# Layer 2's second feed-forward product by seven block products, in groups of six features, with the residual stream added in DRAM

## The chip, the cores and the metric

The kernel runs on one core of a Trainium2 chip. TensorE (PE) multiplies matrices into PSUM, VectorE (DVE), ScalarE (ACT) and GpSimd (POOL) do the rest, and SyncE (SP) issues transfers; ACT and POOL issue some too. Sixteen DMA engines move the data. The metric is the device time of one execution in microseconds (us).

## The reference

One step of a two-layer backbone with residual width 1024: 512 latent tokens and 128 context tokens. Each layer has a mixer and a gated feed-forward part of 2816 hidden units:

```python
def conv_ffn(h, w_up, conv_w, conv_b, w_down):
    a, b = jnp.split(h @ w_up, 2, axis=-1)
    a = dwconv(a, conv_w, conv_b)
    return (jax.nn.silu(a) * b) @ w_down

x = x + g1 * (mix @ p['w_out'][i])
h = rmsnorm(x, p['norm_ffn'][i]) * (1.0 + sc2) + sh2
x = x + g2 * conv_ffn(h, ...)          # after layer 2: y = rmsnorm(x, p['final_norm'])
```

The first product (`w_up`) makes two times 2816 columns, the depthwise convolution runs along the tokens, and the second product (`w_down`) brings the 2816 gated values back to 1024. The gate `g2` has one column for latent and one for context tokens.

## The kernel before

**Layout.** Activations are held with channels on the 128 partitions and tokens along the free dimension: 512 latent tokens, a gap of two columns, 128 context tokens, so 642 columns (`NT`). The residual stream `x` is four tiles of two times 642 columns. The 2816 hidden units are 22 "features" of 128 (`NF`).

**Three matmuls for one.** Every operand of a large product is split into a rounded part and a residue (`fp32r` high and low); `mm3` then issues high x high, low x high and high x low. A split is a cast on ACT and a subtraction on DVE (`split_w`, `split_op`, `Blocks.split`).

**First product (`up_unit`).** The tokens are cut into two halves of 320 (`SPARTS`, `ST`; the gap left out) and the channels into two halves of four. With the two columns of `w_up` that belong to one feature (its `a` and its `b`), this is a two by two block product, done with seven block products instead of eight, of four channel blocks each: 7 x 4 x 3 = 84 matmuls of 320 columns for a feature. `Blocks` and `combine` make the sums and differences of activation blocks, once for the layer; `block_weights` those of the weights for each feature, two of them by a DMA that accumulates (issued on POOL, L591). The seven weight operands use eight half rooms (`op_room`).

**Gate (`give`).** A feature's `a` goes through the convolution (ACT L677, twice DVE L679), SiLU (ACT L683) and the product with `b` (DVE L684), and is split into the tiles of `g` (ACT L686, DVE L687).

**Second product (`project_out`).** The features come in three groups of 8, 7 and 7 (`FGROUPS`). After the up units of a group, each of the eight output blocks takes the group's features as plain products, in two token parts of 384 and 258 columns, and the result times `g2` is added to `x` in SBUF (`residual`, DVE L446). In the last group this carries the final norm with it: squares (ACT L437), their sum over channels, a scaling by the final gain (`scaled`, ACT L2010), and at the end the scaling by the inverse root (`final`, L2020: GpSimd for the first token part, DVE for the second).

**Buffers.** The pool `slots` has 20 slots of 642 x 2 values per partition. In layer 2's feed-forward part 14 hold blocks of activations, 4 hold `x`, 2 the outputs `ab` of the up units. Another pool of 8 slots holds raw blocks at first and the split gated features of one group after that. Raw weights share three buffers (`wr`), the accumulated weight sums two (`t13`).

**Order.** The code is written in program order. The framework's planner gives each engine its own order: it estimates when an instruction's inputs and buffers are there, and of those that are ready takes the one that is written first. Each engine's queue, and that of each transfer issuer, is then fixed and worked off in that order. In the trace weights are so loaded and split about one unit ahead, and matmuls of the next product stand between those of the present one where the plan had a wait.

## Time and profile before

| | us |
|---|---|
| median of 3 runs (1879.08 to 1884.51) | 1882.99 |
| the profiled execution | 1880.43 |
| its span, first to last instruction | 1878.7 |
| layer 2's first up units to its first down stage | 1440 to 1535 |
| the three down stages (8, 7, 7 features) | 1535 to 1592, 1679 to 1729, 1815 to 1867 |
| the tail after the last matmul of the product | 1867 to 1878.7 |

A row of a group reads: line, engine, operation, output and input tiles with their shapes, number, busy time and mean duration of one in nanoseconds, and the idle time before it with what ended it. A row of stages gives the busy time and the number of instructions of each engine, the clock that TensorE was granted (1.00 is full) and the mean busy share of the sixteen DMA engines. A row of the timeline gives start and duration in us. Consecutive matmuls overlap, so the distance of their starts is what one costs.

### The profile page before, as it was taken

The numbers are of one execution on the slowest core, as the hardware profiler recorded it, in microseconds if no ns is written. First come the engines' busy times: TensorE is split into PE (matmuls) and PEld (weight loads), VectorE is DVE, ScalarE is ACT, GpSimd is POOL, SyncE is SP. The second block draws the span as 40 slices with busy tenths as digits, with TensorE's granted clock in tenths as the row PEclk, the third lists the DMA queues.
The fourth block names the chain that finished last, engine by engine and source line by source line (L and its number), as shares of the span: only waits on it lengthen the run. The fifth ranks groups of instructions, "written<-read, shape, count | busy, mean of one in ns | idle before, by whom it ended". The sixth has DMA issues, their size and how long they took to land.

```text
span 1878.7 us, 31471 instructions
## 1 busy us (share of the span) xinstructions
PE 1788.3 (95%) x12052; PEld 1665.0 (89%) x12052; DVE 1374.1 (73%) x2896; ACT 848.1 (45%) x1678; POOL 311.4 (17%) x349
## 2 busy tenths in 40 slices
PE   5899999999888899999999999999999999999997
PEld 1578999998667899999999998977799999999997
DVE  5755666667887989886887888976778874774874
ACT  3555443433232436633634635445526651552653
POOL 2323442324544210000000003200000000000001
PEclk9899999999989999999999999999999999999999
DMA  8332112224544641555556563411242552552631
GB/s 292 128 104 77 36 57 74 67 72 138 176 168 139 234 141 53 143 186 141 138 183 168 130 217 138 140 53 40 91 180 62 146 152 57 146 139 74 160 90 57
DMA packets 86066, 234.20 MB, mean 125 GB/s; under 512 B 9080, under 2 KB 20728, under 8 KB 85786
## 3 DMA queue, kind: packets, MB, share of 16 engines
q1 hardware_dynamic: 66112, 192.45, 30.9%
q0 software_dynamic: 5760, 20.97, 6.7%
q10 hardware_dynamic: 14042, 18.76, 2.9%
q8 instruction: 95, 1.56, 0.3%
q14 instruction: 57, 0.47, 0.1%
HBM read 215.61 MB, written 16.54 MB: 124 GB/s over the span
## 4 chain that ended last, share of the span: by engine, by line
PE 72%; DVE 13%; ACT 3%; POOL 3%; issue 2%; DMA 2%; POOLq 0%; DVEq 0%; ACTq 0%
PE mm L310 10%; PE mm L312 10%; PE mm L311 10%; PE bx L310 4%; PE bx L311 4%; PE bx L312 4%; PE bv L312 2%; PE bv L310 2%; PE bv L311 2%; PE tr L1009 2%; PE fx L1395 1%; PE YT L1176 1%; PE Y L1174 1%; PE Q L1168 1%; PE o L1872 1%
## 5 line engine op out<-in xcount | busy, mean ns | idle before, releaser
L579 ACT CAST cwh<-wr 128x512 fp32r<-128x512 f32 x200 | 119.6, 621 | 144.8 <-PE bx L311 45.9
L304 ACT CAST wwh<-wr 128x1024 fp32r<-128x1024 f32 (+1 forms) x100 | 101.3, 1013 | 175.8 <-PE mm L311 133.9
L580 DVE TENSOR_TENSOR cwl<-wr,cwh 128x512 fp32r<-128x512 f32 x200 | 133.8, 686 | 36.2 <-ACT cwh L579 36.0
L305 DVE TENSOR_TENSOR wwl<-wr,wwh 128x1024 fp32r<-128x1024 f32 (+1 forms) x100 | 122.2, 1223 | 39.4 <-ACT wwh L304 38.6
L310 PE MATMUL mm<-h0h,wwh 128*128 128x384 f32 (+2 forms) x448 | 148.5, 331 | 0.5 <-DVE d L850 0.2
L446 DVE SCALAR_TENSOR_TENSOR x<-mm,mod,x 128x128 f32<-128x128 f32 (+3 forms) x192 | 77.5, 436 | 95.0 <-PE mm L312 94.8
L311 PE MATMUL mm<-h0l,wwh 128*128 128x384 f32 (+2 forms) x448 | 140.1, 313 | 0.0
L591 POOL DMA_DIRECT2D t<-in_w_up x40 | 34.5, 864 | 633.4 <-DMA t<-in_w_up 150.0
L312 PE MATMUL mm<-h0h,wwl 128*128 128x384 f32 (+2 forms) x448 | 139.3, 311 | 0.0
L257 DVE SCALAR_TENSOR_TENSOR mjunk<-mraw,crow 128x512 f32<-128x512 f32 x192 | 125.3, 685 | 1.9 <-DMA mraw<-in_w_modT 1.4
L310 PE MATMUL od<-owh,h2h 128*128 128x256 f32 x320 | 97.0, 305 | 0.1
L679 DVE SCALAR_TENSOR_TENSOR cv<-ab,par,cv 128x641 f32<-128x641 f32 x88 | 77.7, 883 | 25.2 <-ACT cv L677 24.4
L312 PE MATMUL od<-owh,h2l 128*128 128x256 f32 x320 | 91.5, 289 | 2.1 <-DVE h2l L430 1.3
L311 PE MATMUL od<-owl,h2h 128*128 128x256 f32 x320 | 90.5, 284 | 0.0
L310 PEld LDWEIGHTS mm<-h0h,wwh 128*128 128x128 f32 x448 | 85.3, 190 | 3.7 <-issue 1.8
L1139 POOL TENSOR_TENSOR am<-a,msk 128x512 fp32r<-128x512 f32 x60 | 73.0, 1225 | 92.4 <-PE Q L1168 81.2
L311 PEld LDWEIGHTS mm<-h0l,wwh 128*128 128x128 f32 x448 | 84.8, 189 | 0.5 <-issue 0.2
L312 PEld LDWEIGHTS mm<-h0h,wwl 128*128 128x128 f32 x448 | 84.5, 189 | 0.1
L726 DVE SCALAR_TENSOR_TENSOR cv<-mm,par,cv 128x382 f32<-128x382 f32 (+2 forms) x96 | 52.1, 544 | 32.5 <-ACT cv L720 31.7
L579 ACT CAST cwh<-t 128x512 fp32r<-128x512 f32 x80 | 48.0, 622 | 47.5 <-PE bx L311 17.3
L437 ACT ACTIVATE sq<-x 128x320 f32<-128x320 f32 (+4 forms) x63 | 31.5, 501 | 78.7 <-DVE x L446 64.8
L310 PEld LDWEIGHTS od<-owh,h2h 128*128 128x128 f32 x320 | 60.4, 189 | 4.5 <-issue 4.2
(555 smaller groups left out, 6170.7 us busy)
## 6 DMA issues: line engine op xcount, KB each, us to landing
wr<-in_w_mod SPq DMA_DIRECT2D x48, 512.0 KB, 4.6
wr<-in_w_up SPq DMA_DIRECT2D x48, 512.0 KB, 4.2
mraw<-in_w_modT SPq DMA_DIRECT2D x40, 512.0 KB, 5.5
t<-in_w_up SPq DMA_DIRECT2D x80, 256.0 KB, 3.1
t<-in_w_up POOLq DMA_DIRECT2D x40, 512.0 KB, 5.5
wr<-in_w_in SPq DMA_DIRECT2D x28, 512.0 KB, 3.3
wr<-in_w_dn SPq DMA_DIRECT2D x32, 448.0 KB, 3.5
wr<-in_w_up SPq DMA_DIRECT2D x40, 256.0 KB, 3.7
```

The lines of the kernel that those rows point to most:

```text
L257: nc.vector.scalar_tensor_tensor(out=junk, in0=w[:, c : c + 512], scalar=1.0, in1=rows[m][:, c0 + c : c0 + c + 512], op0=ALU.mult, op1=ALU ...
L304: nc.scalar.copy(hi[:, :K], src)
L305: nc.vector.tensor_tensor(out=lo[:, :K], in0=src, in1=hi[:, :K].bitcast(F32), op=ALU.subtract)
L310: nc.tensor.matmul(ps, l[0](k), r[0](k), start=start, stop=False, skip_group_check=more)
L311: nc.tensor.matmul(ps, l[0](k), r[1](k), start=False, stop=False, skip_group_check=more)
L312: nc.tensor.matmul(ps, l[1](k), r[0](k), start=False, stop=stop, skip_group_check=more)
L446: nc.vector.scalar_tensor_tensor(out=xt[:, a:b], in0=ps[:, a - c0 : b - c0], scalar=mcol(layer, ch, d, m), in1=xt[:, a:b], op0=ALU.mult, o ...
L579: nc.scalar.copy(hi, src)
L580: nc.vector.tensor_tensor(out=lo, in0=src, in1=hi.bitcast(F32), op=ALU.subtract)
L679: nc.vector.scalar_tensor_tensor(out=t[:, c0:c1], in0=ar[:, c0 + s_ : c1 + s_], scalar=w[i], in1=t[:, c0:c1], op0=ALU.mult, op1=ALU.add)
L726: nc.vector.scalar_tensor_tensor(out=t[:, c0:c1], in0=p[:, c0 + s_ - a : c1 + s_ - a], scalar=w[i], in1=t[:, c0:c1], op0=ALU.mult, op1=ALU ...
L1139: eng.tensor_tensor(out=v(out), in0=v(a32), in1=msk[:, lv, :, None, :].broadcast_to([P, 2, 2, P]), op=ALU.mult)
```

## The change

In layer 2 the features now come in groups of 6, 6, 6 and 4 (`BGROUPS`). For the first three the second product is a two by two block product as well: token halves of 320, the group's even and odd features, and two neighbouring output blocks. Seven block products of three feature pairs each (7 x 3 x 3 = 63 matmuls of 320 columns) give one pair of output blocks; there are four such pairs for a group.

- `Gated` takes the place of `Act` for these groups. `put` writes the gated feature into a raw tile by two operations (512 and 128 columns); after each odd feature `combine` makes and splits the blocks a11, a12, a22 and the sums s1 to s4.
- `down_weights` makes the seven weight operands of an output pair: four loads on SP's queue, two accumulating transfers on POOL's, two sums on DVE and seven splits.
- `down_blocks` does the products, gates them (`ga` on what comes out with a plus, `ngate` with a minus) into a tile `o` out of `slots`, and adds `o` to the residual in DRAM by an accumulating transfer on POOL's queue. `o` waits for a slot, and its gap is cleared by a memset on POOL.
- `x` is stored to DRAM (`x2s`) on ACT's queue after layer 2's second norm, and its four slots go to `Gated`. It is read back into the other pool after the second unit of the last group, on SP's queue.
- The last group of four features goes through `project_out` as before, with the final norm.

Layer 1 keeps its groups and its products.

```diff
+BGROUPS = ((0, 6), (6, 6), (12, 6), (18, 4))
...
     def split_op(src):
-        hi, lo = op_room()
+        hi, lo = (t_[:, : src.shape[1], :] for t_ in op_room())
...
+    class Gated:
+        PAIRS = (("a12", "a22"), ("s3", "s1"), ("s4", "s2"))
...
+        def room(self, k):
+            p_ = None if k == 0 and self.first else self.pool
+            for i in range(3):
+                self.t[i, k] = slot(f"{self.s}p", (P, 4, ST), F32R, p_)
+            if k % 2 == 0:
+                self.a11[k] = slot(f"{self.s}q", (P, 4, ST), F32R, p_)
+
+        def put(self, f, src):
+            k, i = divmod(f, 2)
+            if i == 0:
+                self.now = slot(f"{self.s}r", (P, 4, ST), pool=self.pool)
+            r = self.now[:, 2 * i : 2 * i + 2, :].rearrange("p n t -> p (n t)")
+            src(0, 512, r[:, :512])
+            src(PO, NT, r[:, 512:])
+            if i:
+                self.room(k)
+                self.combine(k)
...
+        def combine(self, k):
+            TT, STT = nc.vector.tensor_tensor, nc.vector.scalar_tensor_tensor
+            a11, a21, a12, a22 = (self.now[:, i, :] for i in range(4))
+            h_, l_ = self.parts("a11", k)
+            nc.scalar.copy(h_, a11)
+            self.split(0, k, self.now[:, 2:4, :])
+            TT(out=l_, in0=a11, in1=h_.bitcast(F32), op=ALU.subtract)
+            TT(out=a11, in0=a11, in1=a21, op=ALU.subtract)
+            TT(out=a21, in0=a22, in1=a21, op=ALU.subtract)
+            self.split(1, k, self.now[:, 0:2, :])
+            STT(out=a22, in0=a11, scalar=-1.0, in1=a22, op0=ALU.mult, op1=ALU.subtract)
+            STT(out=a12, in0=a22, scalar=-1.0, in1=a12, op0=ALU.mult, op1=ALU.subtract)
+            self.split(2, k, self.now[:, 2:4, :])
...
+    def down_weights(layer, p, f0, n, pool):
+        TT = nc.vector.tensor_tensor
+        m = n // 2
+        w_a, w_b = (A["w_dn"][layer, 2 * p + i][:, 128 * f0 : 128 * (f0 + n)] for i in range(2))
+        eo = lambda ap: ap.rearrange("p (k i c) -> p i k c", i=2, c=128)
+        t13 = pool.tile([P, 1024], F32, tag="t13", name=nm("t13"), bufs=2)[:, : 128 * n].rearrange("p (i k c) -> p i k c", i=2, c=128)
+        for i, w_ in enumerate((w_a, w_b)):
+            nc.sync.dma_start(t13[:, i], eo(w_)[:, 0])
+        for i in range(2):
+            nc.gpsimd.dma_start(t13[:, i], eo(w_b)[:, i], accum_op=ALU.add)
...
+    def down_blocks(xd, G, layer, f0, n, ngate, pool):
+        m = n // 2
+        for p in range(4):
+            o = slot("o")
+            nc.gpsimd.memset(o[:, :, 512:514], 0.0)
+            ws = down_weights(layer, p, f0, n, pool)
...
+            X, Y = bank("d", "dx"), bank("mm", "dy")
+            product(X, "a11", True)
+            q1 = keep("q1", X, SPARTS[0], ga)
+            product(Y, "a12", True)
+            give(0, Y, SPARTS[0], ga, q1)
+            product(X, "s2", False)
+            u2 = keep("u2", X, SPARTS[0], nb)
+            V = bank("d", "dv")
+            product(V, "s1", True)
+            q5 = keep("q5", V, SPARTS[1], nb)
+            product(X, "s3", False)
+            give(1, X, SPARTS[1], nb, q5)
+            product(V, "s4", False)
+            give(1, V, SPARTS[0], nb, u2)
+            product(X, "a22", False)
+            for a, b, c0 in SPARTS[1]:
+                nc.scalar.activation(o[:, 0, a:b], X[:, c0 : c0 + b - a], AF.Copy, scale=ga[0 if a < PO else 1])
+            nc.gpsimd.dma_start(xd[:, 2 * p : 2 * p + 2, :], o, accum_op=ALU.add)
...
+                if xd is not None and not by_blocks and f == f0 + 1:
+                    for i in range(4):
+                        x[i] = slot("xb", pool=gpool)
+                        nc.sync.dma_start(x[i], xd[:, 2 * i : 2 * i + 2, :])
+            if by_blocks:
+                down_blocks(xd, g, layer, f0, n, ngate, pool)
+                continue
...
+            elif xd is not None:
+                for i in range(4):
+                    nc.scalar.dma_start(xd[:, 2 * i : 2 * i + 2, :], x[i])
```

More of the change, by code (lines that the diff above doesn't have):

```diff
@@ new lines, in ffn_blocks @@
+    def ffn_blocks(x, B, pool, layer, then, post, gstack, pre, lanes=((),) * 4, xd=None):
+        gpool = B.pool
+        groups = BGROUPS if xd is not None else FGROUPS
+        if xd is not None:
+            ngate = perm.tile([P, KD, 2], F32, tag="ngate", name="ngate")
+            nc.vector.tensor_scalar(out=ngate, in0=mod[:, layer, 40:48, :], scalar1=-1.0, scalar2=None, op0=ALU.mult)
+        for gi, (f0, n) in enumerate(groups):
+            by_blocks = xd is not None and gi < len(groups) - 1
@@ L671, in ffn_blocks @@
                 nc.gpsimd.memset(t_[:, :, 512:514], 0.0)
-            g = Act(f"g{layer}{gi}", 4, gpool, gap=False)
+            if by_blocks:
+                g = Gated(f"g{layer}{gi}", gpool, True)
+            else:
+                g = Act(f"g{layer}{gi}", (n + 1) // 2, gpool, gap=False)
             def give(f, ar, br, sign):
@@ L1603, in out_and_blocks @@
         pool = gstack.enter_context(tc.tile_pool(name=f"b{layer}", bufs=2))
-        take, pre = to_blocks(x, layer, B)
+        take, pre = to_blocks(x, layer, B, xd)
         between = rows_beside(LANES[3 * layer], pool)
```

68 lines of the change are left out of this document (61 added, 7 removed).

## The prediction

> **What bounds the kernel now.** First the page's totals and its chain of waits, then who TensorE waits for in layer 2's feed-forward part, then that part stage by stage.
>
> ```profile
> span 1878.7 us, 31471 instructions
> PE 1788.3 (95%) x12052; PEld 1665.0 (89%) x12052; DVE 1374.1 (73%) x2896; ACT 848.1 (45%) x1678; POOL 311.4 (17%) x349
> PE 72%; DVE 13%; ACT 3%; POOL 3%; issue 2%; DMA 2%; POOLq 0%; DVEq 0%; ACTq 0%
> ```
>
> ```profile
> engine line waited for: us in total, times, longest us
> PE bv L312 <- DVE cwl L580: 1.8, 1, 1.8
> PE ss L381 <- ACT sq L437: 1.1, 1, 1.1
> PE rb L403 <- POOL nr L395: 1.0, 1, 1.0
> PE by L310 <- ACT cwh L579: 0.3, 1, 0.3
> PE mm L310 <- ACT g12h L686: 0.2, 1, 0.2
> ```
>
> ```profile
> core 0: us, PE busy (x) PEld busy (x) DVE busy (x) ACT busy (x) POOL busy (x), PEclk, DMA share, GB/s
> 1460.00:1472.00 12.00, 9.93 (x55) 9.20 (x54) 9.86 (x19) 5.51 (x10) 0.11 (x1) 0.86 0.26 77
> 1472.00:1484.00 12.00, 12.00 (x84) 12.00 (x84) 12.00 (x21) 9.00 (x17) 1.67 (x2) 1.00 0.82 208
> 1535.00:1592.00 57.00, 56.92 (x384) 56.52 (x383) 23.72 (x39) 11.45 (x16) 0.10 (x1) 1.00 0.21 65
> 1679.00:1729.00 50.00, 49.86 (x337) 49.44 (x337) 22.39 (x39) 10.50 (x15) 0.10 (x1) 1.00 0.22 70
> 1729.00:1815.00 86.00, 86.00 (x588) 86.00 (x588) 68.51 (x113) 51.06 (x98) 4.70 (x9) 1.00 0.49 129
> 1815.00:1867.00 52.00, 51.82 (x353) 51.20 (x351) 25.73 (x45) 22.84 (x48) 6.72 (x5) 1.00 0.13 42
> ```
>
> From 1440 us to the end TensorE waits 4.4 us; up stages (1729) and down stages (1535, 1679, 1815) are full matmul streams. Matmul time taken off is therefore time gained, unless the new order opens gaps. VectorE is the next engine: 68.51 of 86 us going up, all of 12.00 early in the part.
>
> **The change part by part.** *Matmuls.* A 320-column matmul of an up unit takes 86.00/588 = 0.146 us. The three down stages take 57 + 50 + 52 = 159 us. The new ones: three groups of four output pairs of 7 products x 3 feature pairs x 3 matmuls, 3 x 4 x 63 = 756, so 110.6 us; the last four features go the old way, 4/7 of 50.0 = 28.6 us, plus the 2 us by which the last stage now exceeds the middle one. 141.2 us: **-17.8**.
>
> *Start of a block stage.* A stage starts with a wait for its last feature, which passes through ACT and DVE after the last up matmul. Now that wait is covered: a down product of eight features has seven ready, and the planner lets other outputs' first seven go ahead (56.92 of 57 us busy).
>
> ```profile
> 1535.02 0.31 PE L312 MATMUL bx<-a22h,cwl 128*128 128x320 f32 x1
> 1535.21 1.05 ACT L304 CAST wwh<-wr 128x1024 fp32r<-128x1024 f32 x1 [2.46 <-PE bx L311]
> 1536.17 0.48 ACT L657 COPY ab<-bx 128x192 f32<-128x192 f32 x2
> 1537.55 1.81 DVE L679 SCALAR_TENSOR_TENSOR cv<-ab,par,cv 128x641 f32<-128x641 f32 x2
> 1539.45 0.84 ACT L683 ACTIVATE fs<-cv,par 128x642 f32<-128x642 f32 x1 [1.94 <-DVE cv L679]
> 1540.32 0.83 DVE L684 SCALAR_TENSOR_TENSOR fs<-fs,ab 128x642 f32<-128x642 f32 x1 [0.96 <-ACT fs L683]
> ```
>
> The last matmul starts at 1535.02 and the gated feature is there at 1541.15, 6.1 us later; without the down weight's 1.05 us cast ahead of it, about 5.3. Then `combine` must run for the last pair. What depends on the even feature alone (all of a11) can run earlier. The rest takes turns on ACT and DVE: a cast and a residue for a12 and a22, a subtraction, another cast and residue, two more sums, and the third cast and residue. Their nearest rows, the same operations on the inputs of the up product and on the gated feature:
>
> ```profile
> L528 DVE TENSOR_TENSOR s1l<-s,s1h 128x640 fp32r<-128x640 f32 x2 | 1.6, 820 | 0.2 <-ACT s1h L527 0.2
> L528 DVE TENSOR_TENSOR a22l<-a22r,a22h 128x320 fp32r<-128x320 f32 x1 | 0.5, 484 | 0.0
> L687 DVE TENSOR_TENSOR g12l<-fs,g12h 128x642 fp32r<-128x642 f32 x7 | 5.8, 827 | 1.8 <-ACT g12h L686 1.8
> L527 ACT CAST s1h<-s 128x640 fp32r<-128x640 f32 x2 | 1.5, 730 | 0.0
> ```
>
> a12 is whole 1.5 us after the gate (0.73 + 0.82), s4/s2 some 4.5 us after (three 0.82, three 0.48, a cast). TensorE can meanwhile, from the last up matmul on, do a11 (9 matmuls), two thirds of a12, s1 and s2 (18), and a11 of the next pair (9): 36 x 0.146 = 5.3 us; the eight half rooms for split weights hold no more. The gate is there at 5.3 and a12's cast at 6.1, so it idles about 0.8 us there, and in the following 4 us, in which the last thirds of a12, s1 and s2 and the first of s4 come in one by one, about 1 us more. An idle stretch also slows what follows:
>
> ```profile
> 1463.57 0.63 PE L312 MATMUL bv<-s1h,cwl 128*128 128x320 f32 x1 [1.80 <-DVE cwl L580]
> 1465.07 0.47 PE L312 MATMUL bv<-s1h,cwl 128*128 128x320 f32 x1
> 1465.34 0.47 PE L310 MATMUL bv<-s1h,cwh 128*128 128x320 f32 x1
> 1466.93 0.31 PE L311 MATMUL bx<-s2l,cwh 128*128 128x320 f32 x1
> 1467.09 0.31 PE L312 MATMUL bx<-s2h,cwl 128*128 128x320 f32 x1
> ```
>
> After 1.80 us idle the spacing is 0.27 us until 1466.9, then 0.15; that is 3.1 us at little over half rate, 1.4 us lost (clock 0.86 in that stage). I take 1.8 us idle and 0.8 for a slow clock that comes about every second time: 2.6 x 3 = **+7.8**; ends 0.5 (all covered) and 6 each (products kept strictly in written order). The Trainium skill, "TensorE: Matmul & The Clock Gate", Part 1, lets the clock fall only after an idle window of about 3.4 us; by it the sum would be 5.4 here, not 7.8. The row after 1.80 us decides against it.
>
> *VectorE going up.* Per feature pair `combine` adds three 0.82 and five 0.48, drops two 0.83 and splits two gated products (+0.3): +3.5 us, 1.75 per unit. A unit has 68.51/7 = 9.8 of 12.3 us, so 11.5: still under. The weight splits run about seven products ahead, which absorbs unevenness: **+1.5** over the twelve units of the second and third group, ends 0 and 5. In the first group VectorE is already full (12.00 of 12.00) and TensorE lost time there; two pairs come on top, 7 us, of which the slack after 1484 takes part: **+3**, ends 1 and 7. ACT gets 0.6 us per unit on 51.06/7 = 7.3: covered.
>
> *A pair in steady state* is 63 x 0.146 = 9.2 us. DVE: seven residues and two sums of 384 columns, between the rows of 320 and 640 (0.48 and 0.82), about 0.56 each, and four outputs of at most 320, about 0.4: 6.6. ACT: seven casts of 384, about 0.5 by the 0.73 for 640, and six copies out of PSUM of at most 0.4: 5.9 at most. TensorE covers both by 2.6 us and more; without that cover a pair would last as long as the fuller of the two.
>
> *DMA.* A pair of six features loads 1,920 columns of 128 x 4 bytes plainly (0.98 MB: the even blocks of both outputs, all of the first, the odd ones of the second), accumulates 768 (0.39 MB, in 512-byte pieces, two issues on POOL) and adds 1,284 to the residual in DRAM (0.66 MB, a third issue). Gone are 48 of the 72 residual additions on VectorE, which lay beside matmuls. New too are four stores of x on ACT's queue, once, and four loads before the last group on SP's; these wait for the last adds, and behind them stand the weights of the last units, but they are due after the second of four units, 25 us past the last add.
>
> ```profile
> q1 hardware_dynamic: 66112, 192.45, 30.9%
> q0 software_dynamic: 5760, 20.97, 6.7%
> t<-in_w_up POOLq DMA_DIRECT2D x40, 512.0 KB, 5.5
> wr<-in_w_up SPq DMA_DIRECT2D x40, 256.0 KB, 3.7
> ```
>
> Plain traffic costs 0.309 x 1878.7/192.45 = 3.0 us of all sixteen engines per MB, accumulating 0.067 x 1878.7/20.97 = 6.0. A pair needs 2.9 + 2.4 + 3.9 = 9.2 us: as long as its matmuls. The first pair's loads (5.3) run in the up stage, the last add (3.9) in the next, whose own first loads (about 4) come in: 32 of 36.9 us. The software queue takes its transfers in turn, so a weight sum may stand 4 us behind an add; loads land later, and mostly in time: **+1**, ends 0 and 21 (the rival below). No row shows an add into DRAM; I price it as the nearest, the accumulation into SBUF.
>
> POOL's queue is in order, and an add waits for the pair's last copy; behind it stand later weight sums and the memset of the output tile. Weight sums go out early:
>
> ```profile
> 1508.48 0.33 SPq L589 DMA_DIRECT2D t<-in_w_up  x1
> 1513.62 0.85 POOL L591 DMA_DIRECT2D t<-in_w_up  x1 [11.52 <-DVE wr L599]
> 1522.84 0.31 PE L310 MATMUL bx<-a11h,cwh 128*128 128x320 f32 x1
> ```
>
> The sum is issued 9.2 us before its unit's first matmul, as soon as its buffer is free, so a pair's own sum should stand ahead of the previous pair's add. The third pair's output tile needs the first's slot: copy 0.5, issue 0.85, add 5.5 x 0.66/0.52 = 6.9, together 8.3 us after that pair, while it is first written 9.2 + 2.6 us after. Hidden by 3.5 us, and +3.5 at the least if an add takes twice that. I take 0.
>
> *End.* The scaling of the first half on GpSimd
>
> ```profile
> 1861.16 7.02 POOL L2020 TENSOR_TENSOR y<-y,rb 128x768 f32<-128x768 f32 x4 [1.58 <-ACT rb L410]
> ```
>
> starts four half outputs before the last matmul, which now take 4 x 1.4 us instead of 4 x 2.5, so it ends some 4 us deeper in the tail, beside VectorE's own: **+0.8**, ends 0 and 2.
>
> Sum: -17.8 + 7.8 + 1.5 + 3 + 1 + 0.8 = **-3.7 us**. The profiled execution took 1880.43 us, 2.56 under the median of the runs: 1876.7 there, **1879.3** as a median.
>
> **The rivals.** *Most of the gain arrives*: starts cost 1 us each, the first group 1.5, the end 0.5: -12.8, 1870. For it: TensorE waits 4.4 us in 439 now, across changes of stage too. Against: only 36 matmuls are ready. *VectorE becomes the bound going up*: nine pairs x 3.5 = 31.5 in place of 4.5: +23.3, 1906. It decides from 0.8 us more per unit. For it: 12.00 of 12.00; against: slack from 1484. *The adds into DRAM crowd out the weights* (other side): at twice 6.0 us per MB three adds cost 11.8 us more per group, 44 against 36.9, 7 x 3 = 21 us in place of 1: +16, 1899. It decides from 5.5 us per add (4.9 us spare, three adds) instead of 3.9. The Trainium skill, "DMA: Bandwidth & Descriptors", Anatomy of one DMA, gives 2.0 us + bytes/436 GB/s, which by estimate is 4.7 us of data per pair and no such rival; the rows disagree (20.97 MB in 126 us, 167 GB/s; 5.5 us to landing where it says 3.2). *POOL holds each pair's sum behind the add*: 0.5 + 0.85 + 1.7 + 5.5 + 1.5 = 10 us against 2.6 of cover, 7.5 nine times and 6.5 three times: +87 in all, 1966. The early issue speaks against it.
>
> **How the numbers follow.** Forecast 0.51 (own range 1872 to 1886), full gain 0.24, VectorE 0.10, adds 0.11, POOL 0.04. 0.3%, about what can be told from no change, is 5.6 us. The forecast splits 0.16 faster, 0.30 within, 0.05 slower; VectorE 0.02 within: faster 0.40, within 0.32, slower 0.28. Range 1865 to 1905; the POOL case, most of the adds' and half of VectorE's upper ends lie outside.
>
> **What would show it.** 948 down matmuls instead of 1056; block stages of 37 us plus the start gap; TensorE's waits on `combine`'s casts and residues at three starts, with the clock below 1.00 there; VectorE near 11.5 us per unit. Wrong if pairs last over 9.5 us with TensorE waiting for DVE sums of weights that wait for a DMA (adds or POOL), or if up units last over 12.5 us (VectorE).

## The result and the profile after

The changed kernel takes 1898.95 us (median of four runs, 1892.7 to 1901.88), the kernel before beside it 1881.53 (1879.08 to 1884.51): a ratio of 1.009, 95% interval 1.0063 to 1.0118. It is slower by about 17 us, where 1879.3, a little faster, was forecast. It is almost exactly the 1899 that one rival gave, but comes about by other steps, as will be seen. The profiled execution, the slowest of the four, took 1901.88 us with a span of 1900.1.

From the page of the changed kernel: its totals, and the software DMA queue (packets, MB, share of sixteen engines).

```profile
span 1900.1 us, 31843 instructions
PE 1787.8 (94%) x11944; PEld 1657.8 (87%) x11944; DVE 1427.8 (75%) x3061; ACT 902.5 (47%) x1836; POOL 354.9 (19%) x399
q0 software_dynamic: 17088, 33.58, 10.8%
```

The 108 matmuls are gone (12052 before). TensorE's busy time is as it was, 1787.8 against 1788.3, although 17.8 us of full-speed matmuls have left: what is left takes longer. The next view gives the changed kernel by stage: window and length, then the busy time of each engine with its instructions, the granted clock, the DMA share and GB/s. The first, third and fifth row are the block stages, the second and fourth the six up units after them, the sixth the last four up units.

```profile
1513.70:1561.30 47.60, 41.35 (x256) 38.71 (x255) 31.63 (x62) 25.30 (x58) 9.97 (x14) 0.96 0.76 168
1561.10:1636.50 75.40, 74.72 (x508) 74.10 (x507) 62.36 (x117) 45.32 (x92) 9.53 (x10) 1.00 0.63 151
1636.40:1682.40 46.00, 40.77 (x255) 38.79 (x254) 31.68 (x62) 25.34 (x58) 10.01 (x14) 0.96 0.77 175
1682.20:1756.70 74.50, 74.35 (x508) 74.08 (x507) 62.24 (x116) 45.18 (x92) 9.50 (x10) 1.00 0.64 152
1756.50:1805.30 48.80, 43.16 (x255) 41.31 (x254) 31.59 (x62) 25.29 (x58) 10.13 (x17) 0.90 0.75 166
1805.20:1854.60 49.40, 49.40 (x339) 49.40 (x338) 35.19 (x59) 27.68 (x55) 2.69 (x4) 1.00 0.64 180
```

The up stages are as priced (six units of before are 86.4 x 6/7 = 74.1 us). The three block stages are the loss: 252 matmuls each are 36.9 us, and they last 47.6, 46.0 and 48.8, 31.7 us too long in all.

The first block stage in fifths shows two different halves:

```profile
1513.70:1523.20 9.50, 7.81 (x47) 6.67 (x46) 7.27 (x13) 6.33 (x13) 2.64 (x3) 1.00 0.61 115
1523.20:1532.70 9.50, 9.50 (x53) 9.04 (x53) 6.55 (x14) 4.50 (x11) 0.00 (x0) 0.82 0.15 42
1532.70:1542.20 9.50, 7.64 (x52) 7.38 (x51) 5.53 (x12) 5.33 (x15) 3.49 (x3) 1.00 0.98 180
1542.20:1551.70 9.50, 8.41 (x58) 8.15 (x57) 5.68 (x12) 4.78 (x13) 1.92 (x4) 1.00 1.03 241
1551.70:1561.30 9.60, 7.99 (x53) 7.46 (x53) 6.59 (x12) 4.37 (x11) 1.92 (x4) 1.00 1.03 262
```

A fifth has room for 65 matmuls. The first two lose 18 and 12 of them, 4.4 us, by the start; meanwhile the DMA engines fall nearly idle (0.15). In the last three they are full (0.98 to 1.03), and 33 matmuls, 4.8 us, are lost. (A matmul across a cut counts on both sides, so the fifths give somewhat less than the 10.7 us in all.) The start in the timeline of TensorE, start and length of each matmul:

```profile
1519.09 0.31 PE L314 MATMUL dx<-g10q,cwl 128*128 128x320 f32 x1
1520.70 0.41 PE L312 MATMUL dy<-g10p,cwh 128*128 128x320 f32 x1 [1.30 <-ACT g10p L711]
1524.06 0.47 PE L313 MATMUL dv<-g10p,cwh 128*128 128x320 f32 x1
1526.73 0.32 PE L314 MATMUL dy<-g10p,cwl 128*128 128x320 f32 x1
```

TensorE waits 1.30 us for a cast of `combine`, then takes the last thirds as they come (nine matmuls in the 4.0 us to 1523.24, 2.7 lost), and from there to 1526.73, for 3.5 us, matmuls follow each other at about 0.27 us (1.7 lost): the granted clock from 1523.3 to 1526.7 is 0.50. The second stage has the same wait, 1.31 us for `g11p`, and there the clock stays at 1.00 (1645 to 1652); in the third it is 0.61 from 1765 to 1768. Over the first 63 matmuls, a pair's worth, the three stages lose 4.7, 3.2 and 4.5 us. The Trainium skill, "TensorE: Matmul & The Clock Gate", Part 1, has a window of 3.4 us over which activity is judged, and the slow stretch is about that long; but its condition, an idle window, is again not met here: nine matmuls ran in the 3.4 us before.

The second half in the timeline, issues of transfers on SP's and GpSimd's queues, the first pair's last copy (L802) and the engines that wait:

```profile
1530.04 0.90 SPq L740 DMA_DIRECT2D t<-in_w_dn  x2
1532.78 0.68 ACT L802 ACTIVATE o<-dx,mod 128x192 f32<-128x192 f32 x2
1533.33 2.56 POOL L742 DMA_DIRECT2D t<-in_w_dn  x2 [13.19 <-DMA t<-in_w_dn]
1534.89 1.93 POOL L803 DMA_DIRECT2D x2s<-o  x1
1536.06 0.56 DVE L750 TENSOR_TENSOR wr<-t,wr 128x384 f32<-128x384 f32 x1 [2.59 <-DMA wr<-in_w_dn]
1537.01 0.67 DVE L782 SCALAR_TENSOR_TENSOR o<-dx,ngate,q 128x192 f32<-128x192 f32 x2
1537.73 0.42 PE L312 MATMUL dx<-g10p,cwh 128*128 128x320 f32 x1 [1.86 <-DVE o L782]
1543.39 0.10 POOL L763 MEMSET o<- 128x4 f32 x1 [6.57 <-DMA x2s<-o]
1543.46 0.55 DVE L782 SCALAR_TENSOR_TENSOR o<-dy,mod,q 128x320 f32<-128x320 f32 x1 [2.13 <-DMA x2s<-o]
```

The weights of the third pair are requested at 1530.04, 16 us into the stage, because their buffers were held until then. Their sums go out on GpSimd at 1533.33, and the first pair's add behind them, 1.4 us after the pair's last copy ends. VectorE stands 2.59 us at the third pair's weight sum (L750) for its load; behind it in VectorE's queue stand outputs of the second pair (L782), and for these TensorE waits. The memset of the third pair's output tile (L763) waits for the add, and so does VectorE at that pair's first output. What TensorE waited for from 1427 us to the end, and VectorE from 1500 to 1850 (us in total, times, longest):

```profile
PE dv L312 <- ACT q L776: 7.8, 4, 3.5
PE dx L312 <- DVE o L782: 3.4, 3, 1.9
```

```profile
DVE o L782 <- DMA x2s<-o: 10.6, 3, 5.0
DVE wr L601 <- DMA wr<-in_w_up: 10.5, 6, 2.6
DVE wr L750 <- DMA wr<-in_w_dn: 6.2, 5, 2.6
```

Three more rows of TensorE, 1.3 us each, are the starts. VectorE stands 10.6 us at outputs whose tile an add has not yet left, and 16.7 at weight sums. The wait for `q` on ScalarE is one or the other at second hand, for `q` stands behind a cast of weights that wait for a sum. In three of the four cases, 6.9 of the 7.8 us, that sum was itself held on VectorE behind an output that waited for its tile. The largest, in the third stage:

```profile
1787.45 0.55 DVE L782 SCALAR_TENSOR_TENSOR o<-dy,mod,q 128x320 f32<-128x320 f32 x1 [4.96 <-DMA x2s<-o]
1788.97 0.51 ACT L581 CAST cwh<-wr 128x384 fp32r<-128x384 f32 x1 [3.97 <-DVE wr L750]
1789.80 0.67 ACT L776 ACTIVATE q<-dv,ngate 128x192 f32<-128x192 f32 x2
1790.52 0.63 PE L312 MATMUL dv<-g12p,cwh 128*128 128x320 f32 x1 [3.46 <-ACT q L776]
```

The wait for an output tile thus stops TensorE for longer than the late loads do.

### The profile page after: what moved, and what is told of

Read it like the earlier page. It is cut to its first block, busy times and chain, and to the rows that moved or that the text cites. A ratio compares the mean times of both kernels' runs of the same rounds, so it can differ in the third digit from the quotient of the medians.

```text
span 1900.1 us, 31843 instructions
## 1 busy us (share of the span) xinstructions
PE 1787.8 (94%) x11944; PEld 1657.8 (87%) x11944; DVE 1427.8 (75%) x3061; ACT 902.5 (47%) x1836; POOL 354.9 (19%) x399
## 5 line engine op out<-in xcount | busy, mean ns | idle before, releaser
L581 ACT CAST cwh<-wr 128x512 fp32r<-128x512 f32 (+1 forms) x260 | 150.0, 596 | 155.9 <-PE bx L313 43.1
L582 DVE TENSOR_TENSOR cwl<-wr,cwh 128x512 fp32r<-128x512 f32 (+1 forms) x260 | 166.7, 656 | 45.1 <-ACT cwh L581 44.7
L306 ACT CAST wwh<-wr 128x1024 fp32r<-128x1024 f32 (+2 forms) x84 | 82.7, 986 | 128.8 <-PE mm L313 98.5
L307 DVE TENSOR_TENSOR wwl<-wr,wwh 128x1024 fp32r<-128x1024 f32 (+2 forms) x84 | 100.4, 1197 | 32.1 <-ACT wwh L306 31.4
L581 ACT CAST cwh<-t 128x512 fp32r<-128x512 f32 (+1 forms) x104 | 60.9, 596 | 50.4 <-PE bx L313 16.9
L582 DVE TENSOR_TENSOR cwl<-t,cwh 128x512 fp32r<-128x512 f32 (+1 forms) x104 | 67.9, 655 | 9.3 <-PE dy L314 5.7
L448 DVE SCALAR_TENSOR_TENSOR x<-mm,mod,x 128x128 f32<-128x128 f32 (+3 forms) x120 | 48.4, 435 | 26.1 <-PE mm L314 25.8
```

The costliest lines, as they stand in the source:

```text
L306: nc.scalar.copy(hi[:, :K], src)
L307: nc.vector.tensor_tensor(out=lo[:, :K], in0=src, in1=hi[:, :K].bitcast(F32), op=ALU.subtract)
L448: nc.vector.scalar_tensor_tensor(out=xt[:, a:b], in0=ps[:, a - c0 : b - c0], scalar=mcol(layer, ch, d, m), in1=xt[:, a:b], op0=ALU.mult, o ...
L581: nc.scalar.copy(hi, src)
L582: nc.vector.tensor_tensor(out=lo, in0=src, in1=hi.bitcast(F32), op=ALU.subtract)
```

## The experiments

Each run is compared with the kernel before on the same chip beside it; that one's median lay between 1876.0 and 1881.5 us from group to group, so the ratios are what can be compared. "Stage" is the length of a block stage in the profiled execution, from its first matmul to the next group's first; where an up unit is written ahead of the block products, that unit's matmuls among them are taken off. All edits are to the changed kernel. e1 and y4 leave the adds out, so the first three groups are missing from their residual.

| run | ratio to the kernel before | block stages, us |
|---|---|---|
| changed kernel | 1.009 (1.0063 to 1.0118) | 47.6, 46.0, 48.8 |
| e1_no_add | 1.0038 (1.0022 to 1.0054) | 43.4, 40.8, 42.6 |
| e2_sum_dve | 1.0149 (1.0124 to 1.0174) | 50.8, 49.4, 49.8 |
| e3_early | 1.0126 (1.0105 to 1.0147) | 44.5, 46.1, 47.5 |
| e4_both | 1.0205 (1.018 to 1.023) | 50.3, 48.6, 49.9 |
| e5_memset | 1.017 (1.0151 to 1.019) | 51.7, 49.1, 50.5 |
| e6_slot3 | 1.0177 (1.0139 to 1.0215) | 54.1, 52.0, 52.1 |
| e7_plain | 1.0268 (1.0243 to 1.0293) | 56.2, 55.3, 45.6 |
| e8_plain_early | 1.0205 (1.0183 to 1.0226) | 43.7, 43.4, 44.2 |
| x1_w22 | 1.0141 (1.0115 to 1.0167) | 45.9, 48.5, 49.1 |
| x2_sum2 | 1.0069 (1.0045 to 1.0094) | 44.5, 43.1, 44.1 |
| x3_sum2_early | 1.0164 (1.014 to 1.0187) | 46.0, 48.3, 48.0 |
| x4_sum2_early_ms | 1.0153 (1.013 to 1.0177) | 46.5, 45.6, 47.2 |
| y1_sum2_early2 | 1.0017 (1.0001 to 1.0033) | 39.4, 38.7, 37.9 |
| y2_sum2_early2_ms | 1.0128 (1.0083 to 1.0172) | 43.9, 43.9, 45.0 |
| y3_sum2_slot3 | 1.0078 (1.0055 to 1.0102) | 51.1, 42.5, 43.1 |
| y4_noadd_early2 | 0.9991 (0.9976 to 1.0006) | 37.4, 37.3, 37.5 |
| z1_reload | 0.9983 (0.9967 to 1.0) | 38.5, 38.4, 37.8 |
| z2_reload_store | 0.9959 (0.9942 to 0.9975) | 38.2, 38.3, 37.3 |

The first theory after the result: the start costs some 4 us per stage, and the rest is transfers, weight sums and adds together filling the engines. Its rivals: the start alone, and the order on VectorE.

**e1_no_add: without the adds.**

```diff
-            nc.gpsimd.dma_start(xd[:, 2 * p : 2 * p + 2, :], o, accum_op=ALU.add)
```

> The twelve adds into DRAM are left out, so the first three groups' contribution is missing from the residual; all else of the changed kernel stays. Transfer theory (weight sums and adds together fill the DMA engines in the second half of a block stage, which costs about 6.7 us in each): the block stages fall from 47.6, 46.0 and 48.8 us to 40 to 42, and the time from 1899 to 1878-1884. Start theory alone (the wait for the last feature and the slow clock behind it cost everything): the stages stay at 45 us and more, and the time within 3 us of 1899. Engine-order theory (an output on VectorE stands behind the weight sum that waits): it shrinks only as far as the weight sums land earlier, between the two.

The first block stage of this run in the view by stretches of time, columns as above:

```profile
1509.70:1553.10 43.40, 40.59 (x256) 38.70 (x255) 31.82 (x62) 25.31 (x58) 7.34 (x11) 0.96 0.61 141
```

The stages fall by 4.2, 5.2 and 6.2 us, 15.6 in all, the ratio by 0.0052, about 10 us, with intervals that allow 2 to 18 (the changed kernel's profile is the slowest of its four executions, this one the fastest of ten). The adds, with the waits that they cause, carry half of the excess of the stages; 16.1 us of it are there without them. TensorE's wait for `q` is gone with them, and of its wait for outputs 1.6 us are left, of 3.4.

**e2_sum_dve: weight sums on VectorE instead of by transfers.**

```diff
-        for i in range(2):
-            nc.gpsimd.dma_start(t13[:, i], eo(w_b)[:, i], accum_op=ALU.add)
...
+        a, b = load_raw(w_a, n), load_raw(w_b, n)
+        w12, w22 = b[:, 0:n:2], b[:, 1:n:2]
...
+        TT(out=t1, in0=w11, in1=w12, op=ALU.add)
+        TT(out=t3, in0=w12, in1=w22, op=ALU.add)
```

> The two sums of down weights per output pair are taken on VectorE from the two plainly loaded rows of weights instead of by accumulating transfers. A pair's transfers fall from about 10 to about 6.3 us of all engines (0.79 MB plain at 3.0 us per MB, 0.66 MB added at 5.7 to 6.0), VectorE gets two sums of 384 columns more, 1.1 us on 6.6 of 9.2. Transfer theory: block stages of 40 to 42 us, the start gap left over, and 1879-1885 us. If VectorE's order is what delays the outputs, the stages stay at 46 or lengthen by up to 4 us: 1896-1910.

The transfer theory misses: less to transfer, and stages 1 to 3 us longer. The time fits the other branch, VectorE's order. So the DMA engines' time for the transfers is not what binds as such. Both rows now come through the ring of three `wr` buffers, two per pair, which pointed to the time at which loads may start.

**e3_early: the next group's first up unit ahead of the block products.**

```diff
             for f in range(f1, f0 + n):
                 up_unit(layer, f, B, pool, outs, give)
+                if down:
+                    down()
+                    down = None
+                    outs.append(ab_slot())
...
-                down_blocks(xd, g, layer, f0, n, ngate, pool)
+                down = lambda g=g, f0=f0, n=n: down_blocks(xd, g, layer, f0, n, ngate, pool)
```

> The first up unit of the next group stands ahead of a group's block products instead of behind them; nothing else changes. Start theory: the wait for the last feature is covered by 12 us of up matmuls, the stages lose 4 us each, 1885-1889. Transfer theory: what the start loses is in part time in which the loads run, so the transfers then bind earlier and less than 4 us per stage comes back, 0 to 3; 1890-1899.

**e4_both: e2 and e3 together.**

> Sums on VectorE and the up unit ahead of the block products together. If start gap and transfers are the two causes of the 31.7 us that the three block stages take beyond 36.9 each, both go: stages of 37 to 39 us beside the early unit, 1866-1873 us. If a third thing (VectorE's or ScalarE's order in the steady pairs) holds a share, the stages stay above 40 and the time above 1876.

Both miss on the wrong side in time. In e3 the waits for `combine` at the start are gone from TensorE's list of waits, but another there has grown, from 3.4 us to 15.8:

```profile
PE dx L312 <- DVE o L782: 15.8, 6, 3.5
```

Outputs wait for their tiles. The block stages of e3 are still 4.3 us shorter in all; a loss elsewhere outweighs that: the last up stage, three units by now, takes 43.9 us, where three quarters of the changed kernel's 49.4 are 37.1 (z1 below has the reason). The waits for tiles gave the next theory, that the round trip of an output tile binds: written, added (8.3 us from issue to landing), cleared, written again, with two slots.

**e5_memset: gap columns cleared on VectorE, behind the last output.**

```diff
             o = slot("o")
-            nc.gpsimd.memset(o[:, :, 512:514], 0.0)
...
             give(1, V, SPARTS[0], nb, u2)
+            nc.vector.memset(o[:, :, 512:514], 0.0)
```

> The clearing of the output tile's two gap columns moves from GpSimd ahead of a pair to VectorE behind the pair's last output, so GpSimd's queue (weight sums, adds) no longer stands behind an add that must land first; VectorE still waits for the output tile's slot. Output-slot theory (a pair's outputs wait for the add from two pairs before to land, 8.3 us after its issue): a part comes back, because adds and sums are issued earlier; block stages of 43 to 46 us, 1888-1896. If the wait for the slot costs nothing and the transfers' engine time alone binds: within 3 us of 1899.

Slower, not faster. A row of VectorE's waits says why (L799 is the memset):

```profile
DVE o L799 <- DMA x2s<-o: 14.9, 3, 6.4
```

The memset depends on nothing but the slot, so the planner took it early, and VectorE stood 14.9 us at it for the adds, with everything else behind. GpSimd, which waits 29.9 us at these memsets in the changed kernel, has less behind them.

**e6_slot3: a third slot, all gap columns on VectorE.**

```diff
-            o = slot("o")
+            o = slot("o", pool=G.pool if p == 2 else None)
-            nc.gpsimd.memset(o[:, :, 512:514], 0.0)
...
             give(1, V, SPARTS[0], nb, u2)
+            nc.vector.memset(o[:, :, 512:514], 0.0)
...
-            for t_ in outs:
+            for t_ in outs if xd is None or gi == 0 else ():
...
+        if layer and f in (6, 7, 12, 13, 18, 19):
+            nc.vector.memset(outs[f % 2][:, :, 512:514], 0.0)
```

> The third pair's output tile comes from the pool of the group's tiles, where a slot is free then, and the gap columns of output tiles and of the next groups' ab tiles are cleared on VectorE; transfers are the same in number and size. Output-slot theory: the third pair waits for no add, the fourth for one issued 18 us before; block stages of 41 to 43 us, the start gap left over, 1880-1887. Transfer theory: the same bytes in the same time, stages of 45 us and more, 1894-1900.

Slower again, though no row is left of VectorE's outputs waiting for a tile. Its timeline at the end of the first stage, where 4.20 us of TensorE go:

```profile
1564.34 0.69 DVE L601 TENSOR_TENSOR wr<-t,wr 128x512 f32<-128x512 f32 x1 [6.79 <-DMA wr<-in_w_up]
1565.60 0.67 ACT L777 ACTIVATE q<-dv,ngate 128x192 f32<-128x192 f32 x2
1566.32 0.63 PE L312 MATMUL dv<-g10p,cwh 128*128 128x320 f32 x1 [4.20 <-ACT q L777]
```

VectorE stands at the sum of the *next unit's* weights for a load, ScalarE stands at the cast that follows from it, and `q` of the block product stands behind that cast. The planner had put these ahead of the block's own outputs. TensorE's two longest waits, 6.4 us in the second stage and 6.7 in the third, look otherwise. VectorE ahead of the latter:

```profile
1804.27 0.55 DVE L582 TENSOR_TENSOR cwl<-wr,cwh 128x384 fp32r<-128x384 f32 x1 [5.89 <-issue]
1804.29 0.06 DVE L801 MEMSET o<- 128x4 f32 x1
```

VectorE is idle 5.89 us (5.56 in the second stage) up to a residue that the memset of an output tile follows at once, 10.2 us after the first pair's add went out at 1794.03, and soon after it stands 2.58 us more at a weight sum for a load. The profile names no releaser for the idle time; that it is e5's wait at a memset over again is likely, not shown. So e6 does not test the slot alone: its edit also moves the memsets to VectorE.

**e7_plain: plain stores, added up later from DRAM to DRAM. e8_plain_early: the same with e3.**

```diff
-            nc.gpsimd.dma_start(xd[:, 2 * p : 2 * p + 2, :], o, accum_op=ALU.add)
+            nc.scalar.dma_start(sg[:, 2 * p : 2 * p + 2, :], o)
...
+                if xd is not None and 0 < gi < len(groups) - 1 and f < f0 + 4:
+                    i = f - f0
+                    nc.gpsimd.dma_start(xd[:, 2 * i : 2 * i + 2, :], sgs[gi - 1][:, 2 * i : 2 * i + 2, :], accum_op=ALU.add)
```

> Each pair's output goes by a plain store on ScalarE's queue to a DRAM buffer of its group; what the buffers hold is added to the residual later, DRAM to DRAM in four pieces beside the next group's up units (the third group's into the reloaded tiles in on-chip memory). In the block stages the add's 3.8 us of all engines become 2.0 and its landing 4 to 5 us instead of 8.3. Transfer and output-slot theory both: stages of 41 to 43 us, 1880-1887, unless the later accumulations (3.8 us of all engines each, four per group) hold back the up weights, which shows as up stages above 75.4 us. If neither is the cause: stages unchanged, 1897-1905.

> The plain stores and the first up unit of the next group ahead of the block products. With the output slots relieved the cover of the start should now count: stages of 37 to 40 us, 1868-1877. If something else than start and output slots holds a share (weights' sums, ScalarE's order), the stages stay above 41 and the time above 1878.

e7 misses by far; e8 falls on its second branch, with stages above 41 us. The issues of e7 (KB each, median us from issue to landing):

```profile
sg<-o ACTq DMA_DIRECT2D x12, 642.0 KB, 7.5
```

A plain store of an output tile lands in 7.5 us, hardly sooner than an add (8.3), so the round trip stays; the expected 4 to 5 was wrong. What holds e7 back is something else: VectorE stands 47.8 us at weight sums, 16.7 in the changed kernel, and no row shows an output waiting for a tile. In e8 outputs wait 12.3 us for tiles. The additions in e7's up stages cost there: 77.4, 76.2 and 56.8 us instead of 75.4, 74.5 and 49.4.

**x1_w22: own buffers for the odd blocks.** By then the theory was that the loads start late because two of a pair's loads share a ring of three buffers.

```diff
-        w22 = wpool.tile([P, 1024], F32, tag="wr", name=nm("wr"), bufs=3)[:, : 128 * m].rearrange("p (k c) -> p k c", c=128)
+        w22 = pool.tile([P, 384], F32, tag="w22", name=nm("w22"), bufs=2).rearrange("p (k c) -> p k c", c=128)
...
-                q = pool.tile([P, ST], F32, tag=s_, name=nm(s_), bufs=2)
+                q = pool.tile([P, ST], F32, tag=s_, name=nm(s_), bufs=2 if layer == 0 else 1)
```

> The second output's odd weight blocks get two buffers of their own (paid for by one instead of two buffers for each copy kept out of PSUM in this part) instead of the ring of three that they share with the first output's row; nothing else changes. Buffer-ring theory: with three buffers and two loads per pair, the odd blocks of a pair are loaded only after the last split of the pair before, some 1.3 us before that pair's last products begin their run of eight splits ahead; landing takes 3.6 to 5.2 us, so each pair loses lead and VectorE stands at the sum with the previous pair's outputs behind it. With own buffers that wait goes: block stages of 41 to 43 us, 1882-1889. Transfer theory (the engines' time binds): stages stay at 46 to 48 us, within 3 us of 1899.

The one wait aimed at is gone: VectorE's L750 waits for no load any more (6.2 us before). No time came of it. VectorE's waits now:

```profile
DVE o L782 <- DMA x2s<-o: 14.8, 3, 5.0
```

The output tiles take 14.8 us (10.6 in the changed kernel), sums of the next units 15.0 (10.5). The theory of the one ring falls: one late transfer was taken away, and others cost as much.

**x2_sum2: sums on VectorE, with every load a pair ahead.**

```diff
-        for i in range(2):
-            nc.gpsimd.dma_start(t13[:, i], eo(w_b)[:, i], accum_op=ALU.add)
...
+        b = pool.tile([P, 1024], F32, tag="t13", name=nm("t13"), bufs=2)[:, : 128 * n]
+        nc.sync.dma_start(b, w_b)
...
+        t3 = wpool.tile([P, 1024], F32, tag="wr", name=nm("wr"), bufs=3)[:, : 128 * m].rearrange("p (k c) -> p k c", c=128)
+        TT(out=t3, in0=w12, in1=w22, op=ALU.add)
+        TT(out=w12, in0=w11, in1=w12, op=ALU.add)
```

> Weight sums on VectorE as in the run before with that name, but laid out so that every load runs a pair ahead: the second output's row in the ring of two buffers of the weight sums, the first output's row and one sum, which no transfer writes, in the ring of three. Buffer-ring theory: where sums on VectorE cost 8 us more with both rows in the ring of three, they now gain: stages of 40 to 42 us (start gap left), 1879-1886. If VectorE's extra 1.1 us per pair is what cost there: stages of 48 us and more, 1903 and above.

Stages of 43.9 us in the mean, 10.7 us less in all than in the changed kernel, though 2 each above what was expected; the ratios' intervals still overlap. Against e2, the same arithmetic but for the order of two sums, and the same bytes: 6 us per stage, by the buffers. VectorE's wait for output tiles falls from 10.6 us to 0.8. The extra sums on VectorE thus were not what cost in e2.

**x3_sum2_early** (x2 and e3) and **x4_sum2_early_ms** (and e5).

> The same with the next group's first up unit ahead of the block products. If start gap and buffers are all, the stages come to 37 to 39 us (36.9 of matmuls), 1867-1876. If the adds' landing (8.3 us) on the output slots then binds: stages of 41 to 44 us and TensorE waiting for VectorE's outputs, 1880-1892.

> As before it, with the output tiles' gap columns cleared on VectorE behind the last output instead of on GpSimd ahead of the first. If GpSimd's queue standing behind a landing add still costs anything, 2 to 6 us less than the run without it; otherwise within 3 us of it.

Both slower than x2, and within 3 us of each other, which is x4's second branch. For x3, a row of VectorE's and one of TensorE's waits, L779 being the output:

```profile
DVE o L779 <- DMA x2s<-o: 26.4, 6, 5.8
PE dx L312 <- DVE o L779: 17.8, 6, 4.2
```

The second expectation, that the adds' landing binds, is what these rows show, though the stages are 4 to 5 us longer than it had them. The edit of e3 is the reason: the early unit's `ab` tile is kept through the block stage for the units after it, so only one slot was left for output tiles.

**y1_sum2_early2: the early unit with an ab tile of its own.**

```diff
-            outs = [slot("ab") for _ in range(2)]
...
+            outs = 2 * abs_(1) if down else abs_(2)
...
                 if down:
                     down()
                     down = None
-                    outs.append(ab_slot())
+                    outs = abs_(2)
```

> Sums on VectorE in the new layout, the next group's first up unit ahead of the block products, and that unit with an ab tile of its own, which is free again after it, so that two slots are left for the output tiles (one in the earlier try). Output-slot theory: VectorE's 26 us of waiting for adds to land fall below 8, stages of 38 to 41 us, 1870-1881. If the adds crowd out loads whatever the slots: stages of 45 us and more, 1900 and above.

The stages fall from 47.4 us in the mean to 38.7, and both rows of x3 are gone: VectorE waits for no output tile. One slot was worth 8.8 us per stage. This is the clearest of the comparisons, for the tiles alone differ: the add takes a like time to land in both (8.1 and 8.5 us median from issue).

**y2_sum2_early2_ms: y1 and e5.**

> As the one before, with the output tiles' gap columns cleared on VectorE behind the last output. If GpSimd's queue behind a landing add holds the next adds back: 2 to 6 us less than y1; else the same within 3 us.

Neither branch: 5.6 us per stage worse than y1, as e5 was 3.0 worse than the changed kernel. VectorE stands 9.3 us at the memset.

**y3_sum2_slot3: x2 and e6.**

> Sums on VectorE in the new layout, written order kept, a third slot for the third pair's output and all gap columns cleared on VectorE. Start gap left over (4 us per stage): if the output slots and GpSimd's queue are what is left of the adds' cost, stages of 41 to 42 us instead of 44, 1881-1886; if the engines' time is (adds, sums of the next units and loads in the stage's second half), 43 to 45 us as without the third slot, 1888-1893.

The second and third stage are 0.6 and 1.0 us shorter than in x2, the first 6.6 longer. There VectorE stands 6.34 us at the sum of the next unit's weights for a load (L601, up to 1552.86), ScalarE's next cast behind it until 1553.66, the copy `u` of the block product behind that cast, and TensorE waits 5.57 us for `u`. With the written order kept, the slots were no longer what bound.

**y4_noadd_early2: no adds, and the start covered.**

> The twelve adds are left out (the first three groups' contribution is missing from the residual) and the next group's first up unit stands ahead of the block products; weight sums by accumulating transfers as in the changed kernel. If start and adds are the whole of the 31.7 us: stages of 37 to 38.5 us (36.9 of matmuls), 1868-1874. If a third cause holds a share: stages of 40 us and more, 1877 and above.

Its first block stage in the view by stretches of time:

```profile
1523.30:1560.70 37.40, 37.40 (x254) 37.04 (x254) 28.77 (x59) 24.08 (x55) 7.33 (x11) 1.00 0.74 173
```

A full stream at full clock, and in all three stages within 0.6 us of the matmuls, the DMA engines at 0.74. Start and adds make up all but 1.5 of the 31.7 us. Weight sums by transfers do no harm there; beside the adds, with the start covered and two slots, they were not run.

**z1_reload and z2_reload_store.** In y1 the last up stage took 45.0 us, where y4 had 39.2. The timeline of y1 there:

```profile
1799.76 0.33 SPq L870 DMA_DIRECT2D xb<-x2s  x1
1800.18 4.62 SPq L301 DMA_DIRECT2D wr<-in_w_up  x2
1802.01 0.64 PE L312 MATMUL bv<-s4h,cwh 128*128 128x320 f32 x1 [4.62 <-ACT q L637]
```

The last reload of the residual waits on SP's queue for the last add, and the next unit's weights are behind it. z1 writes the reload one unit later; z2 also moves the four stores of x:

```diff
-                if xd is not None and not by_blocks and f == f0 + 1:
+                if xd is not None and not by_blocks and f == f0 + 2:
...
-            elif xd is not None:
-                for i in range(4):
-                    nc.scalar.dma_start(xd[:, 2 * i : 2 * i + 2, :], x[i])
...
                 combine(B, 0)
                 next(us[0], None)
+                if xd is not None:
+                    for i in range(4):
+                        nc.sync.dma_start(xd[:, 2 * i : 2 * i + 2, :], x[i])
```

> y1 with the reload of the residual written behind the third unit of the last group instead of the second. If the reload's wait for the last add held the weights back, the last up stage falls from 45.0 us to 39 to 41 and the time by 4 to 6 us, to 1874-1876 where y1 had 1879.7 (ratio 0.998 to 1.000 of the kernel before). If the last adds' own engine time held them, it stays at 44 and more.

> z1 with the four stores of the residual on SP's queue behind the first plain unit instead of on ScalarE's queue behind the norm. If the stores on ScalarE's queue cost the 3 us between the mixer's last matmul and the first up matmul (66.3 us before, 69 to 70 in every changed kernel), that stretch falls to 66 to 67 us and the time to 1871-1874 (ratio 0.996 to 0.999). If not: within 2 us of z1.

The last up stage of z1 is 37.6 us, shorter than the 39 to 41 expected if the reload's wait was the cause. For the stores, the stretch from the mixer's last matmul to the first up matmul, in the kernel before, in the changed kernel and in z2:

```profile
1359.90:1426.20 66.30, 64.65 (x427) 62.08 (x425) 48.14 (x122) 22.29 (x36) 3.50 (x4) 1.00 0.50 163
```

```profile
1358.40:1427.70 69.30, 66.25 (x433) 63.46 (x431) 51.08 (x132) 25.11 (x41) 5.07 (x8) 0.98 0.61 202
```

```profile
1351.30:1417.60 66.30, 64.66 (x427) 62.07 (x425) 48.10 (x123) 22.49 (x36) 3.50 (x4) 1.00 0.60 201
```

It was 66.3 in the kernel before, is 69.3 in the changed kernel and 69.2 in z1, and 66.3 again in z2: four short issues on ScalarE's queue cost 3 us by these profiles; the intervals of the two runs' times overlap. z2 takes 1868.37 us against 1876.08 for the kernel before beside it, ratio 0.9959 (0.9942 to 0.9975). It is faster than both kernels, by 0.4% than the one before and by about 1.3% (1.009/0.9959) than the changed one.

## Why the prediction was wrong, step by step

**The steps that failed.**

- *The wait for an output tile, 0*, "Hidden by 3.5 us". It is not hidden. The prediction had the third pair's tile free 8.3 us after the first pair and first written 11.8 us after it. In the three stages VectorE came to that output 7.9, 7.1 and 6.5 us after the first pair's last copy, because the second pair's last copy came 5.5 to 6.9 us behind the first's and not a pair's 9.2, and the tile was free only 9.9, 10.5 and 11.4 us after that copy: the add went out 1.3 to 1.4 us late, behind the sums, and took 8.5 to 10.1 us until the memset ran, where 7.8 with its issue was counted. VectorE stood the difference, 10.6 us, and TensorE behind it 1.1, 2.4 and 3.5; in the second and third stage a lower granted clock after that cost some 1.5 and 2.2 more (0.50 from 1790.5 to 1794.0). x3 against y1 shows how dear it gets with one slot less.
- *DMA, +1*: without the adds the stages are 15.6 us shorter (e1), which is this term and the one above together. The bytes were priced well: the software queue's new 12.61 MB took (0.108 x 1900.1 - 0.067 x 1878.7)/12.61 = 6.3 us per MB where 6.0 was taken, and a stage has 0.76 x 47.6 = 36 us of transfers where 32 were counted. The failing was to weigh this against the stage's length as if loads ran evenly. Their buffers held them back in the first half (share 0.15) and they fell together with the adds in the second (1.03). That "loads land later, and mostly in time" was wrong: VectorE stood 16.7 us at weight sums, 9.1 in e1.
- *Start of a block stage, 2.6 x 3 = +7.8*: 12.4 in the changed kernel over the first 63 matmuls of each stage, 16.1 with all else that e1 leaves, which is twice the forecast and within its end of 6 each. Covered, all but 1.5 of it is gone (y4). The order came as foreseen: the first 36 matmuls up to 1519.24, then a wait for the cast. Mis-sized were the piecewise arrivals (2.7 us lost in the first stage instead of 1.8) and the slow clock, which cost 1.7 there, where 1.4 was read, and came in two of three stages instead of every second.
- *Not in the sum:* the stores of x, listed as "four stores of x on ACT's queue, once", were given no price. They cost 3 us (z2).
- *End, +0.8*: measured 3.4. The last down stage lasts 31.4 us (1854.4 to 1885.8) against 30.6 in the sum, and the tail after it 14.3 against 11.7. GpSimd's scaling starts later against the last matmul, as said. The timeline of the changed kernel, and the last matmul of the kernel before:

```profile
1880.62 0.43 DVE L442 TENSOR_TENSOR acc<-acc,sq 128x258 f32<-128x258 f32 x1
1883.38 6.99 POOL L2185 TENSOR_TENSOR y<-y,rb 128x768 f32<-128x768 f32 x4 [1.58 <-ACT rb L412]
1884.10 1.26 DVE L442 TENSOR_TENSOR acc<-acc,sq 128x258 f32<-128x258 f32 x1 [0.55 <-ACT sq L439]
1885.53 0.28 PE L314 MATMUL mm<-g13h,wwl 128*128 128x258 f32 x1
```

```profile
1866.74 0.28 PE L312 MATMUL mm<-g12h,wwl 128*128 128x258 f32 x1
```

The scaling ends 4.6 us after the last matmul (1890.37 against 1885.81); before, that was 1.2. Beside it a sum of VectorE took 1.26 us that took 0.43 ahead of it. That this is why the tail is 2.6 us longer is argued, not shown.

In short, the matmuls' gain came in full, and two terms that were put at 0 and +1, with starts twice as dear, more than took it back. That the median lies within 1865 to 1905 does not speak for the mechanism.

**The steps that held.** Matmuls, -17.8: 948, and y4's stages are 37.4 us. VectorE going up, +1.5: the six-unit stages are 75.4 and 74.5 against 74.1, +1.7; per unit it is 62.4/6 = 10.4 us, below the 11.5 that was forecast, so VectorE is not the bound. First group, +3: 86.2 us against 84.5 that the kernel before takes for its first units less two, +1.7. A steady pair, 9.2 us: 37.4/4 = 9.35 in y4.

The sum with what was measured (16.1 for the starts and what else e1 leaves, 15.6 for the adds): -17.8 + 16.1 + 1.7 + 1.7 + 15.6 + 3.4 + 3.0 = +23.7, against a span 21.4 us longer; 1.4 us less in the part before layer 2's out-projection makes 22.3, so the terms give 0.9 too much.

**The rivals.** *The adds crowd out the weights* gave 1899 and the median is 1898.95. Its place is right, its price is not: it decided by an add of twice the cost, and a megabyte on the software queue costs what the forecast said; the agreement of the two figures is chance. Only half of the stages' excess is the adds at all, and lateness at queues in order makes differences of that size: e2 and x2 have the same transfers and differ by 6 us a stage, x3 and y1 by 8.8, and the add's median landing is much the same in all of them (7.7 to 8.5 us; 8.3 in the changed kernel). *GpSimd holds each pair's sum behind the add*: the other way round, sums stood ahead of the add (1533.33 and 1534.89), and held it. In z2 GpSimd waits 28.5 us at memsets for adds, and it harms nobody. *VectorE going up*: no. "What would show it" named the right sign for wrong, pairs above 9.5 us with TensorE waiting for VectorE and that for a DMA, but had it at weight sums, where the outputs count for more.

**What stays open.** The early unit with two slots was run without the adds (y4) and without the accumulating weight sums (y1), never with both. So it is not shown that the volume of both together, with the DMA share at 1.03, costs nothing. Two repairs made the time worse by what the edit itself did: e3 took a slot, e5 put the memset in VectorE's way; e6 moved memsets along with its slot, so that a third slot alone was not run. Why e7 and x1 are worse, and not only no better, is seen in their rows as an engine standing at a late transfer that the planner had put ahead (in x1 the single buffers for kept copies may have a share). That the planner expects these transfers too early is the reading that fits them; no run changed an estimate. Why the clock fell in two of three stages after the same gap is open too.

## What to carry to other kernels

A balance of transfers over a stage (36 us of work in 47.6) says little; read the DMA share in fifths, and where it is near nothing and then above 1.0, look for the buffers that hold the loads back. Queues are worked off in order, so one late transfer at the head of VectorE's or ScalarE's queue stops outputs that have nothing to do with it; taking away one such wait brings up the next. The time came level with the kernel before (y1) when start, load lead and output slots were mended together, and below it when the reload and the stores were moved too. When a stage begins with a wait for the last product of the stage before, write a unit of the stage after it in between, and see that this does not take a buffer from the stage.

## What the runs showed of the hardware

Not expected: a plain store of a 642 KB tile from on-chip memory to DRAM lands in 7.5 us beside other traffic, an accumulating one in 8.3, so that a store in place of an add shortened the round trip by 0.8 us only. And the granted clock was 0.50 for 3.4 us (1523.3 to 1526.7) soon after a gap of 1.30 us and two of 0.2, less than the 1.80 us that the prediction went by, while in the second stage it stayed at 1.00 after a gap of 1.31 us: the length of a gap alone does not settle it. After the wait of 3.46 us in the third stage it was 0.50 as well. The Trainium skill, "TensorE: Matmul & The Clock Gate", Part 1, calls the queues of ScalarE and VectorE strictly first in, first out; the rows of L750 before L782, and of L601 before `q`, agree.
